# Attention scores in a streaming encoder layer: the high-by-high product as 64-row matmuls on two halves of the array's rows

## The chip, the core and the metric

The kernel runs on one core of a Trainium2 chip. A core has five engines that work side by side: TensorE (PE in the profile, with its weight loads listed apart as PEld), VectorE (DVE), ScalarE (ACT), GpSimd (POOL) and SyncE (SP), and 16 DMA engines. The metric is the device time of one execution in microseconds. Three runs of the kernel before gave 1137.12, 1137.39 and 1137.82 us; the median is 1137.39 us.

## What is computed

One layer of an encoder trunk over 1024 tokens of width 1024: a norm, one input projection that feeds a pooling mixer and a chunked attention, an output projection, a gated MLP, a gated per-layer embedding and a last norm. The change lies in the attention, which is this (cut to one head; 8 heads of width 64, chunks of 64 tokens, each seeing itself and 8 chunks before):

```python
def one_chunk(c, qb):                  # qb: (64 queries, 64)
    kb = slice_of(kp, c * 64, 576)     # 9 chunks of keys
    vb = slice_of(vp, c * 64, 576)
    s = qb @ kb.T * (1 / 8) + bias
    s = where(valid, s, -inf)
    return softmax(s) @ vb
```

## The kernel before

Products are made from split numbers. Each float32 operand is held as a high part, rounded to the narrower format that TensorE takes, and a low part, the remainder. Most products are three matmuls (`mm3`, L126 to L130): high by high, high by low, low by high. TensorE holds one operand (the stationary one, up to 128 rows by 128 columns, brought in by a weight load, LDWEIGHTS) and streams the other through, one column after another. The 128 rows are the contraction.

In the scores the contraction is only 64 long, the width of a head. So the kernel stacks two 64-row parts on top of each other in 128 partitions. Of a head h, with `a` the half of the partitions that its data come from (the lower one for even h, the upper one for odd h) and `b` the other, `qk_stack` (L266 to L284) makes three tiles of 128 by 1024:

- `Q1`: high part of q in half `a` (L276, ACT), low part in half `b` (L277, DVE)
- `K2`: high part of k in half `a` (L279, ACT), low part in half `b` (L280, DVE)
- `K1`: high part of k in half `b` (L281, ACT), low part in half `a` (a copy from `K2`, L282, DVE)

`Q1` by `K2` then gives high by high plus low by low, `Q1` by `K1` gives low by high plus high by low. Two 128-row matmuls give all four products. There are two sets of the three tiles, used by even and odd heads. Each of the six operations is issued once for each half of the tokens, 12 operations a head, as short pieces that are handed out a few at a time between other work (`run_later`).

The attention is a chain over 64 units, 8 heads by 8 tiles of 128 queries. In unit i, `scores(i)` (L333 to L361) multiplies the queries by up to five tiles of 128 keys. A unit with five key tiles ("long" below, the last four or 32 in all) works on 640 columns in two halves of 320, in PSUM banks 4 and 5; a unit with one to four key tiles ("short", the first four of each head, 32 in all) uses one bank and 256, 256, 384 or 512 columns. DVE adds the bias and takes the minimum (L346 or L354), ACT takes the exponential (L356), and DVE or ACT divides by the sum. Two units later `probs_t` (L363) turns the probabilities on TensorE (L370) and splits them (L377, L378); `values` (L380) multiplies them by the values (L387, L388).

TensorE's order is the order in which the program is written. Between the parts of a unit, the loop from L541 on places slices of the projections that come next (`fill`, matmuls of `mm3`). How many go into which unit is worked out ahead by `fill_room` (L78) from a table of assumed times, and the change leaves that table as it is. So on TensorE each unit is a run of matmuls without a gap: scores of unit i, some fill, transposes of unit i - 2, more fill, and in every second unit the values.

The other engines are ordered by a scheduler that follows the order written, except where a priority is given. A long unit's matmuls before:

```python
for z in range(2):
    ks = slice(ki + 320 * z, ki + 320 * z + 320)
    pe.matmul(PS[:, 4 + z, 0:320], q, K2[:, ks], start=True, stop=False)
    pe.matmul(PS[:, 4 + z, 0:320], q, K1[:, ks], start=False, stop=True)
```

Of the kernel before, what the change touches and what calls it, by code (L numbers as in the profile page):

```python
# [9 lines left out]
ALU = mybir.AluOpType  # L10

P = 128
# [5 lines left out]
HD = 64  # L18
# [75 lines left out]
def trunk(tc, xT, pT, vecs, w_qk0, w_in, w_v, bias, counts, pool_w, w_out, w_up, w_down,  # L94
          w_gate, w_ple, out):
    nc = tc.nc
    act, dve, pe, pool, sp = nc.scalar, nc.vector, nc.tensor, nc.gpsimd, nc.sync

    with tc.tile_pool(name="sb", bufs=1) as sb, \
# [8 lines left out]
        PS = pp.tile([P, 8, 512], F32, name="PS")  # L108
# [14 lines left out]
        def rv(ap):  # L123
            return ap.bitcast(F32)
# [141 lines left out]
        def qk_stack(j):  # L266

            Q1, K1, K2 = stacks[j]
            a = slice(HD * j, HD * j + HD)
            b = slice(HD * (1 - j), HD * (1 - j) + HD)  # L270
            q, k = qk32[0], qk32[1]
            todo = []
            for h in range(2):
                z = slice(h * 512, (h + 1) * 512)
                todo += [
                    lambda z=z: act.activation(Q1[a, z], q[a, z], AF.Copy, scale=-0.125),  # L276
                    lambda z=z: dve.scalar_tensor_tensor(Q1[b, z], q[a, z], -0.125, rv(Q1[a, z]),  # L277
                                                         ALU.mult, ALU.subtract),
                    lambda z=z: act.activation(K2[a, z], k[a, z], AF.Copy),  # L279
                    lambda z=z: dve.tensor_tensor(K2[b, z], k[a, z], rv(K2[a, z]), ALU.subtract),  # L280
                    lambda z=z: act.activation(K1[b, z], k[a, z], AF.Copy),  # L281
                    lambda z=z: dve.tensor_copy(K1[a, z], rv(K2[b, z])),  # L282
                ]
            return todo  # L284

# [21 lines left out]
        for t in range(VT0, NTOK):  # L307
            if t < VT0 + 2:
                rstd_rows(t - VT0)
            v_tile(t)  # L310
            v_out(t, 0, v_ps(t))
        later += qk_stack(0)
        run_later(len(later))
        later += qk_stack(1)


# [11 lines left out]
        def keys(i):  # L328
            t = i % NTOK
            k0 = max(0, t - 4)  # L330
            return i // NTOK, t, k0, t + 1 - k0

        def scores(i):  # L333
            h, t, k0, nk = keys(i)
            Q1, K1, K2 = stacks[h % 2]
            b = biasb[h % 2]
            q = Q1[:, t * P:(t + 1) * P]
            S = Sb[i % 3]
            s_ = st[i % 3]
            n, ki = nk * P, k0 * P  # L340
            if nk == BANDT:
                for z in range(2):
                    ks = slice(ki + 320 * z, ki + 320 * z + 320)
                    pe.matmul(PS[:, 4 + z, 0:320], q, K2[:, ks], start=True, stop=False)  # L344
                    pe.matmul(PS[:, 4 + z, 0:320], q, K1[:, ks], start=False, stop=True)  # L345
                dve.tensor_tensor_reduce(  # L346
                    S.rearrange("p (a b) -> p a b", a=2), PS[:, 4:6, 0:320],
                    b.rearrange("p (a b) -> p a b", a=2), 1.0, BIG, ALU.add, ALU.min, s_[:, 0:1])
            else:
                nn = max(n, 256)  # L350
                z = 4 + t % 2
                pe.matmul(PS[:, z, 0:nn], q, K2[:, ki:ki + nn], start=True, stop=False)  # L352
                pe.matmul(PS[:, z, 0:nn], q, K1[:, ki:ki + nn], start=False, stop=True)  # L353
                dve.tensor_tensor_reduce(S[:, 0:n], PS[:, z, 0:n], b[:, 640 - n:640],  # L354
                                         1.0, BIG, ALU.add, ALU.min, s_[:, 0:1])
            act.activation(S[:, 0:n], S[:, 0:n], AF.Exp, bias=s_[:, 0:1], scale=-1.0, accum_out=s_[:, 1:2])  # L356
            dve.reciprocal(s_[:, 2:3], s_[:, 1:2])
            if i % 3 == 0:
                act.activation(S[:, 0:n], S[:, 0:n], AF.Copy, scale=s_[:, 2:3])
            else:  # L360
                dve.tensor_scalar(S[:, 0:n], S[:, 0:n], s_[:, 2:3], None, ALU.mult)  # L361

        def probs_t(i):  # L363
            h, t, k0, nk = keys(i)
            S = Sb[i % 3]
            w = i // 2
# [167 lines left out]
        def stack_up(i):  # L534

            while stacked[0] < N_HEADS and stacked[0] // 2 in qk_ready and i >= (stacked[0] - 1) * NTOK - 1:
                later.extend(qk_stack(stacked[0] % 2))
                stacked[0] += 1

        load_bias(0)  # L540
        for i in range(NI + 3):  # L541
            if i < NI:
                h, t, k0, nk = keys(i)
                if t == 0:
                    while stacked[0] <= h:
                        next(fill)
                        stack_up(i - 1)
                    if h:
                        run_later(len(later))
                    if h + 1 < N_HEADS:  # L550
                        load_bias(h + 1)
                scores(i)
                stack_up(i)
                credit += room[i]
            else:
                credit += DRAIN
# [200 lines left out]
        for z, d in enumerate((0, 4, 1, 5, 2, 6, 3, 7)):  # L757
            k = z // 2
# [264 lines left out]
        for fi in range(4):  # L1023
            up(fi, negative(fi))
            if fi == 0:
# [5 lines left out]
                for s, side in enumerate("wa"):  # L1031
                    for j in range(2):
                        p_ = spots[2 * s + j]
                        pairs[side, j] = p_[:, 0:512], p_[:, 512:1024]
                        for q, kind in enumerate(("one", "grow")):
                            z = 4 * s + 2 * q + j
# [258 lines left out]
```

## Time and profile before

| what | value |
|---|---|
| median of three runs | 1137.39 us (1137.12 to 1137.82) |
| the profiled execution's own time | 1137.53 us |
| its span, first to last instruction | 1135.8 us |
| granted TensorE clock, mean | 0.998 |
| stage with the attention's units | about 55 to 272 us of the span |
| score matmuls L344 and L345 (long units) | 64 each |
| score matmuls L352 and L353 (short units) | 32 each |

The profile records one execution. Busy time of an engine is the time in which at least one of its instructions runs. Matmuls overlap: the next one starts while the results of the one before still leave the array, so a matmul's duration in the list is longer than the distance to the next start, and sums of durations exceed the busy time. PEld is the weight loads; each matmul has one of its own. A row of a group reads: line, engine, operation, output and input tiles, shape and count, then busy time and mean duration. A row of a timeline reads: start in us, duration in us, engine, line, operation.

### The profile page before, as it was taken

The numbers are of one execution on the slowest core, as the hardware profiler recorded it, in microseconds if no ns is written. First come the engines' busy times: TensorE is split into PE (matmuls) and PEld (weight loads), VectorE is DVE, ScalarE is ACT, GpSimd is POOL, SyncE is SP. The second block draws the span as 40 slices with busy tenths as digits, with TensorE's granted clock in tenths as the row PEclk, the third lists the DMA queues.
The fourth block names the chain that finished last, engine by engine and source line by source line (L and its number), as shares of the span: only waits on it lengthen the run. The fifth ranks groups of instructions, "written<-read, shape, count | busy, mean of one in ns | idle before, by whom it ended". The sixth has DMA issues, their size and how long they took to land.

```text
span 1135.8 us, 15750 instructions
## 1 busy us (share of the span) xinstructions
PE 1126.1 (99%) x5675; PEld 956.0 (84%) x5675; DVE 891.0 (78%) x1546; ACT 604.5 (53%) x1071; POOL 143.1 (13%) x188
## 2 busy tenths in 40 slices
PE   9999999999999999999999999999999999999997
PEld 7988998888888888888888888888888888888897
DVE  7678878779658888887788778877887789986854
ACT  8568677765654554444444444444444444674544
POOL 0000000074002200120112011201120112000000
PEclk9999999999999999999999999999999999999999
DMA  7110102103600154575557555755575556420012
GB/s 267 38 50 31 49 13 68 40 29 131 194 19 10 57 151 135 139 174 142 137 155 178 143 130 162 176 145 131 159 171 151 130 152 129 147 93 19 1 75 75
DMA packets 64446, 124.84 MB, mean 110 GB/s; under 512 B 7280, under 2 KB 8560, under 8 KB 64368
## 3 DMA queue, kind: packets, MB, share of 16 engines
q1 hardware_dynamic: 50400, 98.60, 25.9%
q0 software_dynamic: 13824, 25.17, 13.6%
q8 instruction: 44, 0.72, 0.3%
q14 instruction: 34, 0.28, 0.1%
q10 hardware_dynamic: 144, 0.07, 0.0%
HBM read 109.13 MB, written 14.68 MB: 109 GB/s over the span
## 4 chain that ended last, share of the span: by engine, by line
PE 92%; DVE 3%; issue 2%; ACT 1%; POOL 1%; DMA 0%; SPq 0%; POOLq 0%; DVEq 0%; ACTq 0%
PE PS L128 28%; PE PS L129 28%; PE PS L130 28%; PE PS L370 2%; PE PS L388 1%; PE PS L387 1%; DVE R L134 1%; PE PS L345 1%; PE PS L344 1%; ACT R L133 1%; DMA F<-in_w_qk 0%; PE PS L353 0%; PE PS L352 0%; POOL TB L778 0%; DVE F L760 0%
## 5 line engine op out<-in xcount | busy, mean ns | idle before, releaser
L128 PE MATMUL PS<-R 128*128 128x512 f32 (+1 forms) x1176 | 442.7, 376 | 0.2 <-ACT R L232 0.2
L130 PE MATMUL PS<-R 128*128 128x512 f32 (+1 forms) x1176 | 437.8, 372 | 0.0
L129 PE MATMUL PS<-R 128*128 128x512 f32 (+1 forms) x1112 | 420.1, 378 | 0.3 <-DVE R L233 0.3
L130 PEld LDWEIGHTS PS<-R 128*128 128x128 f32 x1176 | 221.7, 188 | 39.0
L128 PEld LDWEIGHTS PS<-R 128*128 128x128 f32 x1176 | 221.8, 189 | 37.8 <-ACT R L232 0.6
L129 PEld LDWEIGHTS PS<-R 128*128 128x128 f32 x1112 | 209.7, 189 | 37.0 <-DVE R L233 0.8
L133 ACT ACTIVATE R<-F 128x512 fp32r<-128x512 f32 (+2 forms) x225 | 140.6, 637 | 173.9 <-PE PS L129 75.2
L134 DVE TENSOR_TENSOR R<-F,R 128x512 fp32r<-128x512 f32 (+2 forms) x221 | 152.8, 701 | 48.3 <-ACT R L133 47.5
L1013 DVE TENSOR_TENSOR F<-F,PS 128x512 f32<-128x512 f32 x140 | 92.6, 682 | 5.8 <-PE PS L130 5.6
L133 ACT ACTIVATE BQ<-RW 128x512 fp32r<-128x512 f32 x90 | 52.6, 622 | 81.1 <-PE PS L129 77.1
L703 DVE TENSOR_TENSOR F<-F 128x512 f32<-128x512 f32 x88 | 60.7, 689 | 39.0 <-DMA F<-in_w_up 37.2
L956 POOL DMA_DIRECT2D RW<-Yd x56 | 49.0, 875 | 260.3 <-DMA RW<-Yd 201.4
L956 POOL DMA_DIRECT2D RW<-in_w_down x40 | 35.5, 941 | 233.5 <-DMA RW<-in_w_down 189.7
L134 DVE TENSOR_TENSOR BQ<-RW,BQ 128x512 fp32r<-128x512 f32 x90 | 59.2, 687 | 1.8 <-PE PS L129 1.3
L356 ACT ACTIVATE F<-F,small 128x640 f32<-128x640 f32 (+2 forms) x64 | 44.4, 693 | 21.3 <-DVE small L354 13.2
L129 PE MATMUL PS<-BQ 128*128 128x512 f32 x140 | 54.6, 390 | 0.1
L130 PE MATMUL PS<-BQ 128*128 128x512 f32 x140 | 54.5, 389 | 0.0
L128 PE MATMUL PS<-R,BQ 128*128 128x512 f32 x140 | 54.5, 389 | 0.0
L128 PE MATMUL PS<-BQ 128*128 128x512 f32 x140 | 54.5, 389 | 0.0
L129 PE MATMUL PS<-R,BQ 128*128 128x512 f32 x140 | 54.5, 389 | 0.0
L130 PE MATMUL PS<-R,BQ 128*128 128x512 f32 x140 | 54.5, 389 | 0.0
L839 ACT ACTIVATE F<-F,vec 128x1024 f32<-128x1024 f32 (+1 forms) x25 | 28.6, 1143 | 44.2 <-DVE F L814 40.8
(188 smaller groups left out, 1806.3 us busy)
## 6 DMA issues: line engine op xcount, KB each, us to landing
F<-in_w_up SPq DMA_DIRECT2D x91, 256.0 KB, 4.0
RW<-Yd SPq DMA_DIRECT2D x60, 256.0 KB, 3.7
RW<-Yd POOLq DMA_DIRECT2D x56, 256.0 KB, 4.8
RW<-in_w_down SPq DMA_DIRECT2D x50, 256.0 KB, 2.8
RW<-in_w_down POOLq DMA_DIRECT2D x40, 256.0 KB, 6.0
Yd<-F SPq DMA_DIRECT2D x40, 256.0 KB, 3.1
F<-in_w_in SPq DMA_DIRECT2D x10, 512.0 KB, 3.7
F<-in_xT SPq DMA_DIRECT2D x16, 256.0 KB, 5.8
```

Of the source, the lines that this page charges most:

```text
L128: pe.matmul(ps, ahi, bhi, start=first, stop=False, skip_group_check=more)
L129: pe.matmul(ps, ahi, blo, start=False, stop=False, skip_group_check=more)
L130: pe.matmul(ps, alo, bhi, start=False, stop=last, skip_group_check=more)
L133: both = (act.activation(hi, src, AF.Copy), dve.tensor_tensor(lo, src, rv(hi), ALU.subtract))
L134: dve.tensor_tensor(lo, src, rv(hi), ALU.subtract))
L344: pe.matmul(PS[:, 4 + z, 0:320], q, K2[:, ks], start=True, stop=False)
L356: act.activation(S[:, 0:n], S[:, 0:n], AF.Exp, bias=s_[:, 0:1], scale=-1.0, accum_out=s_[:, 1:2])
L370: pe.transpose(pst[:, j * P:(j + 1) * P], S[:, j * P:(j + 1) * P], ident)
L703: return dve.tensor_tensor(rawu[to], rawu[a], rawu[b], op)
L839: act.activation(y, Gb[:, 2 + a:2 + b], AF.Identity, bias=vec[:, C_CB + fi:C_CB + fi + 1], scale=cw(2))
L956: pool.dma_start(t, src, accum_op=ALU.add)
L1013: dve.tensor_tensor(t, t, PS[:, 4 + d], ALU.subtract if n in (1, 5) else ALU.add)
```

## The change

The contents of the tiles change in two places. The low part of k goes straight into half `a` of `K1` (it was half `b` of `K2`), and half `b` of `K2` now gets a copy of q's high part. `K1` therefore holds what it held: low k in half `a`, high k in half `b`. `K2` holds high k in half `a` and high q in half `b`. `Q1` stays.

In a long unit the two 128-row matmuls `Q1` by `K1`, one for each half of the columns, come first. Then come two matmuls with 64 rows, high q by high k: one on the array's rows 0 to 63, the other on rows 64 to 127, one for each half of the columns. In half `a` the stationary operand is `Q1` and the streamed one `K2`; in half `b` they are `K2` and `K1`. In a short unit the 128-row matmul `Q1` by `K1` is followed by one 64-row matmul on half `a`. The product of low by low is no longer formed.

```diff
-                    lambda z=z: dve.tensor_tensor(K2[b, z], k[a, z], rv(K2[a, z]), ALU.subtract),
+                    lambda z=z: dve.tensor_tensor(K1[a, z], k[a, z], rv(K2[a, z]), ALU.subtract),
                     lambda z=z: act.activation(K1[b, z], k[a, z], AF.Copy),
-                    lambda z=z: dve.tensor_copy(K1[a, z], rv(K2[b, z])),
+                    lambda z=z: dve.tensor_copy(K2[b, z], rv(Q1[a, z])),
...
+            j = h % 2
+            a = slice(HD * j, HD * j + HD)
+            b_ = slice(HD * (1 - j), HD * (1 - j) + HD)
...
                 for z in range(2):
                     ks = slice(ki + 320 * z, ki + 320 * z + 320)
-                    pe.matmul(PS[:, 4 + z, 0:320], q, K2[:, ks], start=True, stop=False)
-                    pe.matmul(PS[:, 4 + z, 0:320], q, K1[:, ks], start=False, stop=True)
+                    pe.matmul(PS[:, 4 + z, 0:320], q, K1[:, ks], start=True, stop=False)
+                for z in range(2):
+                    ks = slice(ki + 320 * z, ki + 320 * z + 320)
+                    rows = a if z == j else b_
+                    q_, k_ = (Q1, K2) if rows == a else (K2, K1)
+                    pe.matmul(PS[:, 4 + z, 0:320], q_[rows, t * P:(t + 1) * P], k_[rows, ks], start=False, stop=True,
+                              tile_position=(HD * z, 0))
...
-                pe.matmul(PS[:, z, 0:nn], q, K2[:, ki:ki + nn], start=True, stop=False)
-                pe.matmul(PS[:, z, 0:nn], q, K1[:, ki:ki + nn], start=False, stop=True)
+                pe.matmul(PS[:, z, 0:nn], q, K1[:, ki:ki + nn], start=True, stop=False)
+                pe.matmul(PS[:, z, 0:nn], q[a], K2[a, ki:ki + nn], start=False, stop=True, tile_position=(HD * j, 0))
```

## The prediction, made before the changed kernel was run

> **What bounds the kernel now.** I read the page first, for the busiest engine and the chain that ended last.
>
> ```profile
> span 1135.8 us, 15750 instructions
> PE 1126.1 (99%) x5675; PEld 956.0 (84%) x5675; DVE 891.0 (78%) x1546; ACT 604.5 (53%) x1071; POOL 143.1 (13%) x188
> ...
> PE 92%; DVE 3%; issue 2%; ACT 1%; POOL 1%; DMA 0%; SPq 0%; POOLq 0%; DVEq 0%; ACTq 0%
> ```
>
> TensorE is busy 99% of the span and is 92% of the chain. A busy PE can still hide waits, so the second view is the stage with the scores by itself, and the third is the list of what PE waited for in the whole execution.
>
> ```profile
> 55.00:272.00 217.00, 216.11 (x1350) 191.31 (x1349) 174.83 (x424) 152.26 (x327) 35.16 (x62) 1.00 0.14 43
> ```
>
> ```profile
> PE PS L216 <- DVE B L214: 1.5, 1, 1.5
> PE PS L370 <- DVE B L378: 0.8, 2, 0.5
> PE PS L129 <- DVE R L233: 0.3, 1, 0.3
> ```
>
> In the row of the stage (55 to 272 us) the columns after its length are the busy times of PE, PEld, DVE, ACT and POOL, then the granted clock (1.00). PE is busy 216.11 of 217.00 us, DVE 174.83 (81%), ACT 152.26 (70%). Inside the stage PE waits for others 0.8 us in all, in front of the transposes L370, and never in front of the scores. So PE time added to the stage or taken from it goes into the total one for one, as long as DVE's 19% of room lasts: a few us of 217.
>
> The fourth view is the timeline of PE, because durations of matmuls overlap there: what one costs is the distance from its start to the next start.
>
> ```profile
> 150.30 0.31 PE L344 MATMUL PS<-R 128*128 128x320 f32 x1
> 150.45 0.31 PE L345 MATMUL PS<-R 128*128 128x320 f32 x1
> 150.60 0.31 PE L344 MATMUL PS<-R 128*128 128x320 f32 x1
> 150.75 0.31 PE L345 MATMUL PS<-R 128*128 128x320 f32 x1
> 150.89 0.28 PE L128 MATMUL PS<-R 128*128 128x256 f32 x1
> ...
> 151.61 0.71 PE L370 MATMUL PS<-ident,F 128*128 128x128 f32 x5
> 152.07 0.36 PE L128 MATMUL PS<-R 128*128 128x256 f32 x1
> 152.28 0.28 PE L129 MATMUL PS<-B,R 128*128 128x256 f32 x1
> 152.39 0.28 PE L130 MATMUL PS<-R 128*128 128x256 f32 x1
> ...
> 153.82 0.28 PE L352 MATMUL PS<-R 128*128 128x256 f32 x1
> 153.94 0.28 PE L353 MATMUL PS<-R 128*128 128x256 f32 x1
> 154.06 0.28 PE L128 MATMUL PS<-R 128*128 128x256 f32 x1
> ```
>
> A long unit (five key tiles) takes 150.89 - 150.30 = 0.59 us on PE for four matmuls, 0.1475 each. A short one with 256 columns takes 154.06 - 153.82 = 0.24 for two. The counts come from the views of the lines:
>
> ```profile
> L344 PE MATMUL PS<-R x64: 302/309/313, 64.0 to 259.5; 128*128 128x320 f32 x64
> L345 PE MATMUL PS<-R x64: 302/309/312, 64.2 to 259.6; 128*128 128x320 f32 x64
> L353 PE MATMUL PS<-R x32: 282/311/396, 55.6 to 248.2; 128*128 128x256 f32 x16, 128*128 128x384 f32 x8, 128*128 128x512 f32 x8
> L248 PE MATMUL PS<-small,F x16: 168/250/250, 34.4 to 36.0; 128*128 128x1 f32 x16
> ```
>
> There are 64/2 = 32 long units and 32 short ones. One matmul lasts 0.309 us where the next starts after 0.1475, so 0.309 - 0.1475 = 0.16 us of each lies under its successors. L248 has one column per matmul, so its distance, (36.0 - 34.4)/15 = 0.107 us, is the least time that a load of 128 columns of weights needs.
>
> **The change, part by part.** Matmuls stay as many: 4 in a long unit, 2 in a short one. The cross product (high by low and low by high) keeps one full 128-row matmul per column half. High by high becomes a 64-row matmul. In a long unit the two of them use different halves of the array's rows and different PSUM banks (4 and 5). Three things can move PE.
>
> *The overlap.* If the two 64-row matmuls of a long unit run at once, one of four distances goes: 32 x 0.1475 = 4.72 us is the most that this change can give, since nothing in a short unit has a partner. Whether it is reached depends on the loads.
>
> ```profile
> 152.05 0.19 PEld L128 LDWEIGHTS PS<-R 128*128 128x128 f32 x1
> 152.07 0.36 PE L128 MATMUL PS<-R 128*128 128x256 f32 x1
> 152.16 0.19 PEld L129 LDWEIGHTS PS<-B,R 128*128 128x128 f32 x1
> 152.28 0.28 PE L129 MATMUL PS<-B,R 128*128 128x256 f32 x1
> 152.28 0.19 PEld L130 LDWEIGHTS PS<-R 128*128 128x128 f32 x1
> ```
>
> The load for the next matmul starts as the present one starts (152.28 and 152.28). Call the four matmuls of a unit M1 to M4. M3's load starts with M2 and M4's load can follow 0.107 later, so M4 starts 2 x 0.107 = 0.214 after M2, while M3 starts after 0.1475. The unit then takes 0.1475 + 0.214 + 0.1475 = 0.509 instead of 0.59, a gain of 0.081 us, times 32 = 2.6 us. If M4's load starts only when M3 does, M4 is 0.107 behind M3, the unit takes 0.5495 and the gain is 0.0405 x 32 = 1.3 us. If the two don't overlap at all, it is 0. So the overlap lies between 0 and -4.72 us.
>
> *The switch of the array's shape.* Each unit goes once from 128-row to 64-row matmuls and once back, long or short: 64 x 2 = 128 switches. The trace of before has no 64-row instruction, so the price d of a switch is bounded from the nearest rows. The low bound is the change to transposes and back: five of them and the L128 behind take 152.28 - 151.61 = 0.67 us, where 5 x 0.107 + 0.12 = 0.655 would be their plain distances; 0.015 for two changes, so about 0.008 each. The high bound is that a switch lets everything in the array finish: the 0.16 us by which a matmul outlasts its distance. A gain from switching is excluded: it removes no instruction. I take the middle, 0.085 us, since a transpose keeps all 128 rows and is not really a change of shape, while 0.16 includes the reading of operands, which need not wait.
>
> With d = 0.085, M3 starts 0.1475 + 0.085 = 0.2325 after M2, later than the 0.214 at which both loads are in, so the pair overlaps fully. A long unit takes 3 x 0.1475 + 2 x 0.085 = 0.6125, +0.0225 against 0.59; times 32 = +0.7 us. A short unit pays 2 x 0.085 = 0.17 and gets nothing back; times 32 = +5.4 us. Sum +6.2 us. At d = 0.008 and the overlap limited by loads the sum is 32 x (3 x 0.008 - 0.081) = -1.8 us; at d = 0.16 it is 32 x (0.32 - 0.1475) + 32 x 0.32 = +15.8 us. The sign turns where 3d = 0.081, at d = 0.027 us (with the overlap complete at no cost, at 4.72/128 = 0.037).
>
> A rule of the Trainium skill speaks against this change: "TensorEngine Tiling (Array Packing)", Key Properties, says that going over to another tiling mode, as opposed to another tile of the same mode, drains TensorE. It gives no time for it; no run here shows it yet, and the sum above goes by rows alone.
>
> *The stacks.* Three rows and one engine's waits bear on them.
>
> ```profile
> L280 DVE TENSOR_TENSOR R<-F,R x16: 683/685/689, 44.1 to 213.6; 64x512 fp32r<-64x512 f32 x16
> L281 ACT ACTIVATE R<-F x16: 629/630/634, 44.3 to 213.6; 64x512 fp32r<-64x512 f32 x16
> L282 DVE CAST R<-R x16: 413/421/424, 45.3 to 214.4; 64x512 fp32r<-64x512 f32 x16
> ```
>
> L280 keeps its shape and writes to K1's other half instead of K2's; L282 copies Q1's high half instead of K2's low half, at the same size. Count, engines and sizes stay, so I cost both at nothing; were each to differ by as much as 0.02 us, 32 of them make 0.6 us on DVE, hidden by its 42 us of free time in the stage and worth 0.6 us without it. L282 newly needs ACT's L276, but L280, ahead of it on DVE, already needs L279, which ACT runs after L276. No wait is added, and nothing queues behind one. M1 now needs L280 and L281, M3 and M4 need L282, where M2 needed L282 before; PE has no wait there. No DMA moves.
>
> The profiled execution took 1137.53 us, 1.7 more than its span and 0.14 above the median of 1137.39; the 6.2 us are added to the median: **1143.5 us**.
>
> **The rivals.**
>
> *Faster: a switch costs next to nothing and the pairs overlap.* From -2.6 us (load-limited, 1134.8) to -4.7 (1132.7). For it: 0.015 us around the transposes, and PE so tight that every ns shows. Against it: half the units pay for switches with no partner to gain from, so 0.027 to 0.037 us a switch is enough to lose it. The Trainium skill, "TensorE: Matmul & The Clock Gate", Part 3, states that matmuls on different row groups start about 4 ns apart and run concurrently; no run here shows it, and by it the result is this rival's far end.
>
> *It doesn't do what it says.* The 64-row matmuls run one behind the other, or M4's load waits for M3's start, with cheap switches: between 0 and -1.3 us, 1136.1 to 1137.4. For it: in every row above a matmul starts only when the one before has streamed its columns. Against it: no row has two matmuls on different rows.
>
> *Slower by far: a switch drains the array and holds back the loads too.* The place is the first load of the new shape, and the price 0.16 + 0.107 = 0.267 us for each of 128 switches; 34.2 - 4.7 = +29.5 us, 1166.9. For it: 84% busy PEld, so loads have little slack. Against it: loads start ahead of their matmul everywhere in the trace. It decides from the point where a load can't start before the older shape is out.
>
> **How the numbers follow.** What a measurement of this kernel can tell from no change is about 0.2%, 2.3 us. The forecast (d from 0.03 to 0.16, the pair overlapping) has 0.46, the rival with held-back loads 0.07, the faster rival 0.33, the one without overlap 0.14. Of the forecast's own range, 1138 to 1153.2, about 0.04 lies within 2.3 us of before. So faster 0.33, same 0.14 + 0.04 = 0.18, slower 0.42 + 0.07 = 0.49. The likeliest one's own range is 1138 to 1153. The wide range goes from the complete overlap at no switch cost (1132.7, rounded down to 1132.5) to some us above the drain at 0.16 (1153.2; 1156 with a little of the loads held back); outside are the worst rival and little else.
>
> **What would show it.** In the timeline of a short unit, the distance from the 64-row matmul to the next full one, and from the full one to the 64-row one, is the price of each switch: 0.12 for 256 columns means none, about 0.2 means 0.085. In a long unit, the starts of M3 and M4: under 0.03 apart is full overlap, 0.07 to 0.11 the loads, 0.15 none. The rows of L280 and L282 should keep 0.69 and 0.42 us, PE should stay over 99% busy in the stage, and all other stages should keep their lengths. Wrong would be a time under 1137, which says that d lies below 0.027; or one above 1156, which says that loads wait too. A change outside 55 to 272 us would show a mechanism that I don't have.

## The result, and the profile after

The changed kernel takes 1154.8 us (median of 4 runs, 1154.34 to 1155.62) against 1137.36 us before on the same chip: 17.4 us more, a ratio of 1.015 with a 95% interval of 1.0138 to 1.0162. Run once more, beside other runs of the kernel before, it gave 1155.03 against 1138.70, a ratio of 1.0148 (1.0133 to 1.0164). Slower was forecast, with +6.2 us; the loss is 2.8 times that.

The page of the changed kernel, the rows that answer to those of before:

```profile
span 1152.6 us, 15751 instructions
PE 1143.9 (99%) x5675; PEld 953.8 (83%) x5675; DVE 892.7 (77%) x1546; ACT 605.0 (52%) x1071; POOL 142.9 (12%) x188
...
PE 93%; DVE 3%; issue 2%; ACT 1%; POOL 1%; DMA 0%; SPq 0%; POOLq 0%; DVEq 0%; ACTq 0%
```

PE is busy 17.8 us longer, with the same 5675 matmuls; PEld, DVE, ACT and POOL keep their sums within 2.2 us. So it is not other work that grew, but what PE's work takes. The time of the same stage of the kernel (its columns as before: PE, PEld, DVE, ACT, POOL):

```profile
55.00:289.00 234.00, 234.00 (x1345) 188.82 (x1344) 176.54 (x423) 153.41 (x328) 34.77 (x62) 1.00 0.13 40
```

Cut at 289 us instead of 272, the stage holds nearly the same matmuls (1345 against 1350), so it is about 17 us longer, at the same clock of 1.00. Laid beside the trace of before, the rest of the execution is 0.6 us shorter. Now the timelines of PE and of PEld around one long unit, at 148.68 us:

```profile
148.56 0.28 PE L396 MATMUL PS<-B,R 128*128 128x256 f32 x1
148.68 0.46 PE L347 MATMUL PS<-R 128*128 128x320 f32 x2
149.07 0.41 PE L352 MATMUL PS<-R 64*128 64x320 f32 x2
149.41 0.39 PE L128 MATMUL PS<-R 128*128 128x256 f32 x1
149.64 0.28 PE L129 MATMUL PS<-B,R 128*128 128x256 f32 x1
```

```profile
148.56 0.31 PEld L347 LDWEIGHTS PS<-R 128*128 128x128 f32 x2
149.07 0.19 PEld L352 LDWEIGHTS PS<-R 64*128 64x128 f32 x2 [0.19 <-issue]
149.41 0.19 PEld L128 LDWEIGHTS PS<-R 128*128 128x128 f32 x1 [0.16 <-issue]
149.52 0.19 PEld L129 LDWEIGHTS PS<-B,R 128*128 128x128 f32 x1
149.64 0.19 PEld L130 LDWEIGHTS PS<-R 128*128 128x128 f32 x1
```

This is the whole story, read in order. The two full matmuls L347 start at 148.68 and 0.147 later; they have streamed at 148.68 + 2 x 0.1475 = 148.975. In the kernel before the next load would have begun with the second of them. Here the two loads of L352 begin at 149.07 only, 0.095 after the old shape has streamed, with PEld idle for 0.19. Then the loads take their time in the open, with no matmul streaming beside them. The x2 in 0.19 us says that both loads run side by side, and so do the two matmuls, which start 0.003 us apart in the trace; for the two loads of L347 the row has 0.31. The way back is the same: L128's load begins at 149.41, and the load for L129, which starts when L128's columns do, at 149.52, 0.11 later. From the unit's first start to L129 it is 149.64 - 148.68 = 0.96 us; before it was 0.59 + 0.12 = 0.71. A switch costs (0.96 - 0.71 + 0.147)/2 = 0.20 us: about 0.09 until the load may begin and 0.107 for the load.

A short unit has two switches and no pair:

```profile
54.90 0.28 PE L360 MATMUL PS<-R 128*128 128x256 f32 x1
55.10 0.38 PE L361 MATMUL PS<-R 64*128 64x256 f32 x1
55.41 0.50 PE L128 MATMUL PS<-R 128*128 128x512 f32 x1
55.75 0.39 PE L129 MATMUL PS<-R 128*128 128x512 f32 x1
```

From L360 to L129 it is 0.85 us, where 0.24 for the unit and 0.23 for a matmul of 512 columns make 0.47: 0.38 for two switches, 0.19 each.

PE's order is the same in both kernels, matmul for matmul, so the two traces can be laid side by side. Summed over all units (from a unit's first start to the second start behind it), in us:

```
kernel                        32 long units   32 short units   between the units
changed kernel                     +8.0            +11.9            -2.4
```

The sum of +17.5 less 0.6 that a faster start happened to give is the 16.9 by which this execution's own time, 1154.39, stands above 1137.53. The -2.4 is waits at the transposes that went away: 2.3 of it lies at the starts of transposes. In the view of the transposes' line, the idle time of PE and PEld together, before (L370) and after (now L378), the last two figures being us and times:

```profile
its engine sat idle before it (us, times) until:
  DVE B L378: 5.0, 12
```

```profile
its engine sat idle before it (us, times) until:
  issue: 1.7, 7
  DVE B L386: 0.6, 2
```

Of the 5.0 us before, PEld has 4.2 in 10 waits and PE 0.8 in two of the same places; after, all of it is PEld's. So DVE's split of the probabilities (L378 before, L386 after) is late ten times before and twice after: with PE slower, DVE is mostly in time.

### The profile page after: what moved, and what is told of

The parts are those of the page before. It is cut to its first block, busy times and chain, and to the rows that moved or that the text cites. A ratio compares the mean times of both kernels' runs of the same rounds, so it can differ in the third digit from the quotient of the medians.

```text
span 1152.6 us, 15751 instructions
## 1 busy us (share of the span) xinstructions
PE 1143.9 (99%) x5675; PEld 953.8 (83%) x5675; DVE 892.7 (77%) x1546; ACT 605.0 (52%) x1071; POOL 142.9 (12%) x188
## 4 chain that ended last, share of the span: by engine, by line
PE 93%; DVE 3%; issue 2%; ACT 1%; POOL 1%; DMA 0%; SPq 0%; POOLq 0%; DVEq 0%; ACTq 0%
PE PS L128 29%; PE PS L129 28%; PE PS L130 27%; PE PS L378 2%; PE PS L396 1%; PE PS L395 1%; DVE R L134 1%; PE PS L361 1%; PE PS L352 1%; PE PS L347 1%; ACT R L133 1%; PE PS L360 0%; DMA F<-in_w_qk 0%; POOL TB L786 0%; DVE F L768 0%
## 5 line engine op out<-in xcount | busy, mean ns | idle before, releaser
L128 PE MATMUL PS<-R 128*128 128x512 f32 (+1 forms) x1176 | 446.5, 380 | 0.2 <-ACT R L232 0.2
L129 PE MATMUL PS<-R 128*128 128x512 f32 (+1 forms) x1112 | 419.7, 377 | 0.3 <-DVE R L233 0.3
L128 PEld LDWEIGHTS PS<-R 128*128 128x128 f32 x1176 | 221.6, 188 | 43.7 <-issue 4.5
L129 PEld LDWEIGHTS PS<-R 128*128 128x128 f32 x1112 | 209.6, 189 | 36.8 <-DVE R L233 0.6
L134 DVE TENSOR_TENSOR R<-F,R 128x512 fp32r<-128x512 f32 (+2 forms) x221 | 152.8, 702 | 45.5 <-ACT R L133 44.1
L134 DVE TENSOR_TENSOR BQ<-RW,BQ 128x512 fp32r<-128x512 f32 x90 | 59.1, 685 | 2.2 <-PE PS L129 1.7
L129 PE MATMUL PS<-BQ 128*128 128x512 f32 x140 | 54.6, 390 | 0.1
L128 PE MATMUL PS<-R,BQ 128*128 128x512 f32 x140 | 54.5, 389 | 0.0
L129 PE MATMUL PS<-R,BQ 128*128 128x512 f32 x140 | 54.5, 389 | 0.0
L128 PE MATMUL PS<-BQ 128*128 128x512 f32 x140 | 54.5, 389 | 0.0
```

Of the source, the lines that this page charges most:

```text
L128: pe.matmul(ps, ahi, bhi, start=first, stop=False, skip_group_check=more)
L129: pe.matmul(ps, ahi, blo, start=False, stop=False, skip_group_check=more)
L134: dve.tensor_tensor(lo, src, rv(hi), ALU.subtract))
```

## The experiments

The theory is that a change of the array's shape costs about 0.195 us in either direction, whatever is computed, and that the pair on two row halves overlaps fully. The rivals are that the new order of the products costs the time, that each 64-row matmul is dear by itself, and that the pair doesn't overlap. Each time below is a median, with that of the kernel before on the same chip.

**The order alone.** The stacks and the 128-row matmuls of before, in the new order:

```diff
-                    pe.matmul(PS[:, 4 + z, 0:320], q, K2[:, ks], start=True, stop=False)
-                    pe.matmul(PS[:, 4 + z, 0:320], q, K1[:, ks], start=False, stop=True)
+                    pe.matmul(PS[:, 4 + z, 0:320], q, K1[:, ks], start=True, stop=False)
+                for z in range(2):
+                    ks = slice(ki + 320 * z, ki + 320 * z + 320)
+                    pe.matmul(PS[:, 4 + z, 0:320], q, K2[:, ks], start=False, stop=True)
...
```

The two matmuls of a short unit change places in the same way.

> The kernel before, with its stacks and its 128-row matmuls, but the order of the changed kernel: K1 for both halves, then K2 for both halves. Theory (a change of the array's shape costs about 0.195 us, 0.09 until the load may start and 0.107 for the load itself): nothing changes, 1137.4 us. Rival (the order of the products and its waits cost the time): most of the 17.4 us, about 1150.

Measured: 1137.80 against 1137.67, ratio 1.0003 (0.9993 to 1.0012). The order costs nothing that can be told from noise.

**Long units alone.** The upper half `b` of `K2` gets the low part of k for the first 512 tokens and the high part of q for the last 512. Short units read only the first, long units take their queries from the last, so both forms fit:

```diff
-                    lambda z=z: dve.tensor_copy(K2[b, z], rv(Q1[a, z])),
+                    lambda z=z, h=h: dve.tensor_copy(K2[b, z], rv((K1, Q1)[h][a, z])),
...
-                pe.matmul(PS[:, z, 0:nn], q[a], K2[a, ki:ki + nn], start=False, stop=True, tile_position=(HD * j, 0))
+                pe.matmul(PS[:, z, 0:nn], q, K2[:, ki:ki + nn], start=False, stop=True)
```

> Row groups in the long units only; the short units have their 128-row matmuls back. Theory: 64 switches and 32 overlapped pairs, 32 x (2 x 0.195 - 0.147) = +7.8 us, less up to 2.4 that waits before the transposes give back: 1142.8 to 1145.2. Rival (each 64-row matmul is dear by itself, 17.4 us over 96 of them): 64 of them, +11.6 us, 1149.0.

Measured: 1145.23 against 1137.67, +7.6 us, ratio 1.0063 (1.0048 to 1.0078). The time is inside the forecast, but partly by luck: PE's list of waits has one of 1.5 us for DVE's L134, which neither the kernel before nor the changed one has. By the trace, 8.0 us more in the long units and this wait, less 2.0 us that went away between the units, make it up.

**Short units alone.** The stacks and long units of before; the second matmul of a short unit with 64 rows:

```diff
...
-                pe.matmul(PS[:, z, 0:nn], q, K2[:, ki:ki + nn], start=True, stop=False)
-                pe.matmul(PS[:, z, 0:nn], q, K1[:, ki:ki + nn], start=False, stop=True)
+                pe.matmul(PS[:, z, 0:nn], q, K1[:, ki:ki + nn], start=True, stop=False)
+                pe.matmul(PS[:, z, 0:nn], q[a], K2[a, ki:ki + nn], start=False, stop=True, tile_position=(HD * j, 0))
```

> 64-row matmuls in the short units only; the long units and the stacks are those of before. Theory: 64 switches and no pair, 64 x 0.195 = +12.5 us, less up to 2.4: 1147.5 to 1149.9. Rival (each 64-row matmul is dear by itself): 32 of 96, +5.8 us, 1143.2.

Measured: 1149.0 against 1137.67, +11.3 us, ratio 1.0097 (1.0082 to 1.0112). A third of the 64-row matmuls costs more than the other two thirds, as the theory has it: the same 64 switches without the pairs. Side by side with the trace of before, the long units of the one kernel are 8.0 us longer, the short ones of the other 11.8, which are the two sums of the changed kernel (8.0 and 11.9).

**Twice the switches in a long unit.** The same matmuls as in the changed kernel, in the order full, 64 rows, full, 64 rows:

```diff
                     pe.matmul(PS[:, 4 + z, 0:320], q, K1[:, ks], start=True, stop=False)
-                for z in range(2):
-                    ks = slice(ki + 320 * z, ki + 320 * z + 320)
```

> The changed kernel with the long unit's matmuls in the order full, 64 rows, full, 64 rows: same matmuls, four switches instead of two and no pair side by side. Theory: 32 x (4 x 0.195) + 32 x 2 x 0.195 - 2.4 = +35 us, 1172.5. Rival (each 64-row matmul is dear by itself): their number is the same; at most the lost overlap is added, 1154.8 to 1159.5.

Measured: 1171.51 against 1137.67, +33.8 us, ratio 1.0299 (1.0284 to 1.0315). This kills the rival of the dear 64-row matmul. PE's timeline of one of its long units:

```profile
158.01 0.31 PE L347 MATMUL PS<-R 128*128 128x320 f32 x1
158.25 0.41 PE L350 MATMUL PS<-R 64*128 64x320 f32 x1
158.59 0.41 PE L347 MATMUL PS<-R 128*128 128x320 f32 x1
158.93 0.41 PE L350 MATMUL PS<-R 64*128 64x320 f32 x1
159.27 0.38 PE L128 MATMUL PS<-R 128*128 128x256 f32 x1
```

Behind each switch the next one is 0.34 us away, 0.1475 of streaming and 0.19, from 64 rows to 128 as from 128 to 64.

**No pair.** Both 64-row matmuls of a long unit on the same half of the rows:

```diff
-                    rows = a if z == j else b_
-                    q_, k_ = (Q1, K2) if rows == a else (K2, K1)
-                    pe.matmul(PS[:, 4 + z, 0:320], q_[rows, t * P:(t + 1) * P], k_[rows, ks], start=False, stop=True,
-                              tile_position=(HD * z, 0))
+                    pe.matmul(PS[:, 4 + z, 0:320], q[a], K2[a, ks], start=False, stop=True,
+                              tile_position=(HD * j, 0))
```

> The changed kernel with both 64-row matmuls of a long unit on the same half of the rows, one behind the other; switches as in the changed kernel. Theory (the pair overlaps fully in the changed kernel): 32 x 0.147 = +4.7 us, 1159.5. Rival (the pair does not really run side by side): no difference, 1154.8. If the second load is not hidden under the first matmul, 32 x 0.107 = 3.4 us more, 1162.9.

Measured: 1159.68 against 1138.11, +21.6 us, ratio 1.0184 (1.0167 to 1.0201); the changed kernel had +17.4. The 4.1 us between them (21.57 less 17.44) is the overlap, 0.13 for each of 32 pairs; in the trace a long unit is 0.392 us longer than before, against 0.250 in the changed kernel, 0.142 apart. PE's rows of one of its long units, and PEld's:

```profile
151.58 0.46 PE L347 MATMUL PS<-R 128*128 128x320 f32 x2
151.97 0.56 PE L350 MATMUL PS<-R 64*128 64x320 f32 x2
152.46 0.39 PE L128 MATMUL PS<-R 128*128 128x256 f32 x1
```

```profile
151.97 0.29 PEld L350 LDWEIGHTS PS<-R 64*128 64x128 f32 x2 [0.19 <-issue]
```

On the same rows two 64-row matmuls take 0.56 us and their two loads 0.29, where the pair on two halves takes 0.41 and 0.19. The pair overlaps almost completely.

**All 64 rows.** A long unit as three pairs:

```diff
-                for z in range(2):
-                    ks = slice(ki + 320 * z, ki + 320 * z + 320)
-                    pe.matmul(PS[:, 4 + z, 0:320], q, K1[:, ks], start=True, stop=False)
+                for step in range(2):
+                    for rows in (a, b_):
+                        z = rows.start // HD
+                        ks = slice(ki + 320 * z, ki + 320 * z + 320)
+                        pe.matmul(PS[:, 4 + z, 0:320], q[rows], K1[rows, ks], start=step == 0, stop=False,
+                                  tile_position=(rows.start, 0))
```

> A long unit wholly in 64-row matmuls, three pairs; of the cross products each half of the columns takes one twice and leaves the other out. The unit has six 64-row matmuls instead of two, and still two switches. Theory (switches set the price): as the changed kernel, 1154.8, within 2 us. If two loads on different rows go one after the other, 0.214 for each pair against 0.147 of streaming, 32 x 2 x 0.067 = +4.3 us, 1159.1. Rival (each 64-row matmul is dear by itself, 0.18 us): 32 x 4 x 0.18 = +23 us, less the saved full ones, above 1168.

Measured: 1156.19 against 1138.11, +18.1 us, ratio 1.0156 (1.0141 to 1.0171): the price of the changed kernel within 0.7 us, with three times the 64-row matmuls in a long unit. In the trace a long unit, counted from the start of the matmul ahead of it, is 0.249 us longer than before, against 0.250 in the changed kernel. PE's timeline of one:

```profile
149.51 0.28 PE L399 MATMUL PS<-B,R 128*128 128x256 f32 x1
149.72 0.56 PE L349 MATMUL PS<-R 64*128 64x320 f32 x4
150.12 0.31 PE L355 MATMUL PS<-R 64*128 64x320 f32 x2
150.35 0.38 PE L128 MATMUL PS<-R 128*128 128x256 f32 x1
```

From 149.72 to 150.35 it is 0.63 us: 0.107 for the first loads, 3 x 0.147 for three pairs, and 0.09. So loads of pairs that follow one another are hidden, as those of full matmuls are. This run also meets one more rival, that the wait comes from adding to what matmuls of the other shape have just written to a PSUM bank: here the first 64-row matmuls begin a new sum (`start=True`), and still they start 0.21 us after L399, which streams for 0.12.

**Four pairs in one visit.** If switches set the price, fewer visits with more pairs should turn the sign. From the kernel with row groups in long units alone:

```diff
-                    pe.matmul(PS[:, 4 + z, 0:320], q, K1[:, ks], start=True, stop=False)
-                for z in range(2):
+                    pe.matmul(PS[:, 4 + z, 0:320], q, K1[:, ks], start=True, stop=t < 7)
+                for n_, z in [(n_, z) for n_ in range(4) for z in range(2)] if t == 7 else ():
...
-                    pe.matmul(PS[:, 4 + z, 0:320], q_[rows, t * P:(t + 1) * P], k_[rows, ks], start=False, stop=True,
+                    pe.matmul(PS[:, 4 + z, 0:320], q_[rows, t * P:(t + 1) * P], k_[rows, ks], start=False, stop=n_ == 3,
...
```

> Short units as before; of the four long units of a head, the first three leave out their high-by-high product, and the last takes its own four times, as four pairs in one visit to the 64-row shape. Two switches a head instead of eight, the same number of pairs: what merging visits could give at most. Theory: 8 x (2 x 0.195 - 4 x 0.147) = -1.6 us, 1135.8, or up to 1137.3 if the wait of 1.5 us that the kernel with row groups in long units alone shows stays. A visit with four pairs should take 0.195 + 4 x 0.147 + 0.195 on PE. Rival (pairs behind one another don't run side by side, since the loads can't keep up): 8 x (0.39 + 4 x 0.067) = +5 us, above 1140.

Measured: 1141.13 against 1138.70, ratio 1.0022 (1.0013 to 1.0031). The time missed: +2.4 us where -1.6 was expected, and by the time alone the rival's +5 is the nearer. The timeline of a visit says otherwise:

```profile
151.37 0.46 PE L347 MATMUL PS<-R 128*128 128x320 f32 x2
151.76 0.86 PE L352 MATMUL PS<-R 64*128 64x320 f32 x8
152.55 0.39 PE L128 MATMUL PS<-R 128*128 128x256 f32 x1
```

From the first load (151.76) to that of L128 (152.55) it is 0.79 us: 0.107 for the first loads, 4 x 0.147 for eight matmuls in four pairs, and 0.09. One behind the other they would have needed 1.18 for the streaming alone. Laid beside the trace of before, the scores of a typical head are 0.2 us shorter on PE (three units 0.293 shorter, the last 0.688 longer, by the medians); summed over all 32 long units it is -1.3 us, near the -1.6 expected. What the theory of the kernel lacked is in PE's list of waits:

```profile
PE PS L378 <- DVE B L386: 3.1, 7, 0.7
PE PS L216 <- DVE B L214: 1.5, 1, 1.5
PE PS L129 <- DVE B L134: 1.4, 1, 1.4
```

The transposes now wait 3.1 us for DVE's L386 where it was 0.8 before, and one projection matmul waits 1.4 us for its weights' low part (L134, also DVE); that second wait is in the kernel with row groups in long units alone, too, with 1.5 us. So -1.3, the 2.3 us more before the transposes and 1.4 make the +2.4. The first wait fits a reading by which PE time taken out of units where DVE sets the pace turns into waits, which no run tests by itself. The second has another source, since PE is slower in the kernel with row groups in long units alone: in both, DVE runs one L134 behind an L386 and an L264 (at 133.21 us here), where it ran ahead of them in the kernel before (at 131.37 us). Both share the edit of L282's copy; that this edit moved L134 isn't shown. A table of fill made for the new times might give part of it back; that wasn't tried, and a kernel that holds four units' scores to merge their visits would need eight PSUM banks for scores where two are free for them. No version was found that beats the kernel before.

**The changed kernel again**, on the same chip as the last:

> The changed kernel once more, beside the same runs of the kernel before: 1154.8, 17.4 above it.

Measured: 1155.03 against 1138.70, +16.3 us, ratio 1.0148 (1.0133 to 1.0164); the 17.4 lies within this interval.

## Why the prediction was wrong in size

The direction held, and so did the parts of the sum; the price of a switch was mis-sized, since the load of the new shape was taken to be hidden. The 1154.8 us lie above the forecast's own 1138 to 1153 and only inside the wide range, whose upper end allowed for loads that are held back a little. Point by point:

- *PE sets the time, and only in 55 to 272 us.* Right. The length of the span moved by 16.8 us and that of the stage by 17.5.
- *The overlap, 0 to -4.72 us, taken as complete.* Right: 4.1 us by the kernel without the pair, 4.5 by its trace (32 x 0.142), and both loads go side by side, which the working had thought to need 0.214 us one after the other.
- *128 switches, two in each unit, short ones with no gain.* Right, shown by the two half changes (+7.6 and +11.3 us) and by twice the switches in a long unit (+33.8).
- *The price d = 0.085 us.* This step failed: it is 0.195. The part before the load, about 0.09, is nearly the value taken, by luck: that was the middle between 0.008 and 0.16, and no run shows how much of the 0.16 is the reading of operands. The error is the sentence that M3 starts "later than the 0.214 at which both loads are in": loads were taken to run ahead across a switch, as they do between matmuls of one shape. They don't; the load starts about 0.09 us after the last column of the old shape, and its 0.107 us lies open. With 0.195 the same sum is 32 x (0.39 - 0.1475) + 32 x 0.39 = 7.8 + 12.5 = 20.2 us.
- *The rival with held-back loads* (0.07) had this mechanism and the wrong price, 0.267, since it took the whole 0.16 of a matmul's tail for the part before the load. Its objection, that loads start ahead everywhere in the trace, came from a trace without any switch.
- *PE time goes into the total one for one.* Off by 2.4 us the other way. PE's own list of waits showed 0.8 us in the stage, but PEld's idle time before the transposes was 4.2 us, and a slower PE won back about 2.4 us there. So 20.2 - 2.4 = 17.8 us, against 17.4 measured.
- *The stacks at nothing, no new wait.* Right: L280 and L282 keep 0.684 and 0.422 us, and PE's list of waits has no new entry after the change. (The order alone, with the stacks of before, gave a ratio of 1.0003.)

The rule of the Trainium skill that was weighed, "TensorEngine Tiling (Array Packing)", Key Properties, says that a change of tiling mode drains TensorE. The trace agrees with it in part: the first load of the new shape waits 0.09 us behind the last column of the old, but it starts (149.07) 0.07 us before the record of the last old matmul ends (148.68 + 0.46 = 149.14). The profile models these ends, so whether the array is empty by then isn't shown.

## What to carry to other kernels

Two matmuls on two halves of the rows run side by side, so the pair is worth one streaming time, here 0.147 us. A visit to another array shape costs two switches, here 0.39 us, so by these figures it pays only from three pairs of this size on, and never for a matmul without a partner. Four pairs in a visit did take PE time away, about 0.2 us a head, but the waits took more back, and no run shows a gain in the whole time. When a term has no row in the trace, ask of each thing that is hidden today whether it would still be hidden behind the new operation, and price it open as well.

## What the runs showed of the hardware

- A weight load for another shape begins about 0.09 us after the last matmul of the old shape has streamed its columns; between matmuls of one shape it begins as the matmul before does (152.28 and 152.28 in the rows of before). Both directions cost the same, about 0.19 to 0.20 us with the load, and for 256 and 320 columns alike.
- Two loads for different halves of the rows run side by side: 0.19 us for both in the row of L352, where two full loads one after the other show 0.31 and two loads for the same half 0.29.
- Going over to transposes and back costs nothing like it (0.015 us for both, in the rows of before); the transposes use all 128 rows.
